# Gate and up products of a decoder layer's two SwiGLU FFNs with the tokens on the partitions

## The chip, the cores and the metric

The kernel runs on one core of a Trainium2 chip, as one launch. The metric is the time of one execution on the device in microseconds, the median of several runs. Engines: PE is TensorE's matmul, PEld its weight load (the load of the stationary operand), DVE is VectorE, ACT is ScalarE, POOL is GpSimd, SP is SyncE, whose queue issues the DMAs.

## What is computed

One decoder layer on 256 tokens of width 2048, in float32: a SwiGLU FFN (half step), a token mixer, a second SwiGLU FFN (half step). Each sub-layer has an RMSNorm with shift and scale ahead of it, an RMSNorm with a gate behind it, and a residual.

```python
def swiglu(h, w_gate, w_up, w_down):
    return (jax.nn.silu(h @ w_gate) * (h @ w_up)) @ w_down

mod = (jax.nn.silu(c) @ w_ada[l] + b_ada[l]).reshape(b_, N_SUBLAYERS, N_MOD, D_MODEL)

def sublayer(x_res, j, fn, coef):
    shift, scale, gate = mod[:, j, 0], mod[:, j, 1], mod[:, j, 2]
    h = rms_norm(x_res, g_pre[l, j]) * (1.0 + scale[:, None, :]) + shift[:, None, :]
    y = rms_norm(fn(h), g_post[l, j])
    return x_res + coef * gate[:, None, :] * y
...
x = sublayer(x, 0, ffn(0), 0.5)
x = sublayer(x, 1, mixer, 1.0)
x = sublayer(x, 2, ffn(1), 0.5)
```

w_gate and w_up are 2048 x 5632, w_down is 5632 x 2048, for each of the two FFNs. w_ada, from which the shifts, scales and gates come, is 2048 x 18432.

## The kernel before

Products are made in three parts. Every operand is split into a high part (rounded to fp32r by a cast) and a low part (what the cast left), and `mm3` (lines 308 to 311) sums high x high, high x low and low x high in PSUM. The activations h lie transposed in SBUF as `hh` and `hl`: 128 partitions by 16 k's by 256 tokens. A weight tile is two k's by 512 columns: `load_w` (line 277) loads it over SP's queue into one of 8 `raw` buffers, `split_w` casts it on ScalarE to `wh` (line 290) and subtracts on VectorE to `wl` (line 291), with 4 buffers each. `w_tiles` (line 295) hands out the tiles of a product; after each tile it calls `pump`, which takes one step of the first of the `pending` generators (evacuations and the like), and lets a side generator step, which loads the next piece of w_ada and sums it on VectorE (line 170).

An FFN works in 11 blocks of 512 columns of w_gate and w_up, taken together in three supers of 4, 4 and 3 blocks, each followed by its part of the down products. A block needs two products, gate and up, each with 8 weight tiles. `proj_t` (line 319) makes them with the output channels on the partitions: the weight tile is the stationary operand, 128 columns at a time, and h moves with its 256 tokens; for one k that is 4 x 3 matmuls of 256 columns into two PSUM banks. `proj_tok` (line 333) is the other form: h is stationary, 128 tokens at a time, and the weight tile moves with 512 columns, 2 x 3 matmuls for a k. The projections of the mixer go by `proj_tok`, but for the two that the convolution reads. In the FFNs only the first block of the second FFN does, since its products are begun while half of the tokens are still in work.

The first FFN begins before h is complete: blocks 0 to 4 get their first quarter of the k's, blocks 5 and 6 a half, block 7 three quarters, and `spill` (line 649) copies each of these sums out of PSUM (line 651). Between them the generator `First` makes shift and scale of the next quarter. The blocks are finished later, and `swiglu_sum` (line 514) adds the spilled part. Block 8 keeps its banks.

SwiGLU's result g must have the channels on the partitions, since the down products use it as the stationary operand. `swiglu_evac` (line 505) takes the silu of the gate's bank, multiplies it by the up's bank (line 509) and splits the result into g (lines 342, 343), one bank per pump. `swiglu_tok` (line 532) does it for the wide block: silu and product of both banks (lines 537, 538), then, at the next two pumps, four transposes each on TensorE against an identity (line 546) into a PSUM bank, and the split out of that bank.

The order of each engine's instructions comes from a scheduler that follows the order in which the code is written and lets an engine go on with later work whose operands and buffers are free. PSUM has 8 banks in one pool, small tiles `t` have 6 buffers.

Of the kernel before, what the change touches and what calls it, by code (L numbers as in the profile page):

```python
# [9 lines left out]
F32R = mybir.dt.float32r  # L10
AF = mybir.ActivationFunctionType
# [21 lines left out]
def tile_layer(  # L33
# [35 lines left out]
    def ps():  # L69
        return psp.tile([P, 512], F32, tag="ps", name=nm("ps"))  # L70
# [237 lines left out]
    def mm3(o, lh, ll, rh, rl, start, stop):  # L308
        nc.tensor.matmul(o, lh, rh, start=start, stop=False, skip_group_check=True)  # L309
        nc.tensor.matmul(o, lh, rl, start=False, stop=False, skip_group_check=True)  # L310
        nc.tensor.matmul(o, ll, rh, start=False, stop=stop, skip_group_check=True)  # L311
# [4 lines left out]
        slots = [Slot((P, 2, 2, 512), F32R) for _ in range(n - nw)]  # L316
        return list(w_tiles(src, segs, c0, [None] * min(n, nw) + [s_.t for s_ in slots])), slots

    def proj_t(src, c0, segs=FULL, banks=None, first=0):

        banks = banks or [ps(), ps()]
        last = segs[-1][0] + segs[-1][1] - 1
        for k, wh, wl in w_tiles(src, segs, c0):
            for m in range(4):
                o = banks[m // 2][:, (m % 2) * S:(m % 2 + 1) * S]
                mm3(o, wh[:, m * P:(m + 1) * P], wl[:, m * P:(m + 1) * P],
                    hh[:, k, :], hl[:, k, :], k == first and m % 2 == 0, k == last)
        return banks

    def tok_mm(k, wh, wl, t, bank):  # L330
        mm3(bank, hh[:, k, t * P:(t + 1) * P], hl[:, k, t * P:(t + 1) * P], wh, wl, k == 0, k == NK - 1)

    def proj_tok(src, c0, begun=None, w=512):

        banks, done = begun or ([ps(), ps()], 0)
        for k, wh, wl in w_tiles(src, FULL[done:], c0, w=w):
            for t in range(NT):
                tok_mm(k, wh, wl, t, banks[t][:, 0:w])
        return banks

    def split_act(dh, dl, src):
# [160 lines left out]
        return banks, 2  # L502


    def swiglu_evac(g, gb, ub):
        for i in range(2):
            sg, gt = t2(), t2()
            nc.scalar.activation(sg, gb[i], AF.Silu)
            nc.vector.tensor_tensor(out=gt, in0=sg, in1=ub[i], op=ALU.mult)
            split_act(g.t[:, 0, 2 * i:2 * i + 2, :], g.t[:, 1, 2 * i:2 * i + 2, :],  # L510
                      gt.rearrange("p (k s) -> p k s", s=S))
            yield

    def swiglu_sum(gb, ub, part):

        pv = part.t.rearrange("p k s -> p (k s)")
        gts = []
        for i in range(2):
            sg, gt = t2(), t2()
            nc.vector.tensor_tensor(out=sg, in0=pv[:, i * 512:(i + 1) * 512], in1=gb[i], op=ALU.add)  # L520
            nc.scalar.activation(sg, sg, AF.Silu)
            nc.vector.tensor_tensor(out=gt, in0=pv[:, 1024 + i * 512:1024 + (i + 1) * 512], in1=ub[i], op=ALU.add)
            nc.vector.tensor_tensor(out=gt, in0=sg, in1=gt, op=ALU.mult)
            gts.append(gt)
        part.free()
        g = Slot((P, 2, 4, S), F32R)
        for i in range(2):
            split_act(g.t[:, 0, 2 * i:2 * i + 2, :], g.t[:, 1, 2 * i:2 * i + 2, :],
                      gts[i].rearrange("p (k s) -> p k s", s=S))
        return g  # L530

    def swiglu_tok(g, gb, ub):

        gts = []
        for t in range(NT):
            sg, gt = t2(), t2()
            nc.scalar.activation(sg, gb[t], AF.Silu)
            nc.vector.tensor_tensor(out=gt, in0=sg, in1=ub[t], op=ALU.mult)
            gts.append(gt)
        yield  # L540
        for i in range(2):
            pg = ps()
            for j in range(2):
                for t in range(NT):
                    m = 2 * i + j
                    nc.tensor.transpose(pg[:, j * S + t * P:j * S + (t + 1) * P], gts[t][:, m * P:(m + 1) * P], ident)
            split_act(g.t[:, 0, 2 * i:2 * i + 2, :], g.t[:, 1, 2 * i:2 * i + 2, :],
                      pg.rearrange("p (k s) -> p k s", s=S))
            yield

    def ffn(idx, supers, begun, xin, nxt, nxt_src=None, nxt_c0=None, nxt_w=512):

        y = None
        yp = [parts() for _ in range(NT)]

        def evac_y(si, q, t, bank):
            ys = y[t].t[:, q * 512:(q + 1) * 512]
            if si == 0:
                nc.scalar.copy(ys, bank)
            else:  # L560
                nc.vector.tensor_tensor(out=ys, in0=ys, in1=bank, op=ALU.add)
            if si == len(supers) - 1:
                sumsq(yp[t], q, ys)

        for si, blocks in enumerate(supers):
            gs = []
            n = len(blocks)
            for b, segs, part, banks in blocks:
                if si == 0 and begun is not None and not gs:
                    gb = proj_tok(w_ff_gate[idx], b * FB, begun)  # L570
                    ub = proj_tok(w_ff_up[idx], b * FB)
                elif part is not None:
                    gb = proj_t(w_ff_gate[idx], b * FB, segs, None, segs[0][0])
                    ub = proj_t(w_ff_up[idx], b * FB, segs, None, segs[0][0])
                    flush()
                    gs.append(swiglu_sum(gb, ub, part))
                    continue
                else:
                    gb = proj_t(w_ff_gate[idx], b * FB, segs, banks and banks[0])
                    ub = proj_t(w_ff_up[idx], b * FB, segs, banks and banks[1])  # L580
                flush()
                gs.append(Slot((P, 2, 4, S), F32R))
                ev = swiglu_tok if si == 0 and begun is not None and len(gs) == 1 else swiglu_evac
                pending.append(ev(gs[-1], gb, ub))
            if y is None:
                y = [Slot((P, D)) for _ in range(NT)] if xin[0].__class__ is Half else [Half(t) for t in range(NT)]
            rows = [(4 * i, 4, 4 * b[0]) for i, b in enumerate(blocks)]

            def mms(k, wh, wl, t):
                g = gs[k // 4].t  # L590
                mm3(banks[t], g[:, 0, k % 4, t * P:(t + 1) * P], g[:, 1, k % 4, t * P:(t + 1) * P],
                    wh, wl, k == 0, k == 4 * n - 1)

            for q in range(4):
                banks = [ps(), ps()]
                if si == len(supers) - 1 and q == 2:
                    for s_ in xin:
                        s_.t
                if si == len(supers) - 1 and q == 3:
                    flush()  # L600
                    if side[0] is not None:
                        side[0].drain()
                    early = early_w(nxt_src, nxt_c0, nxt_w)
                    kept, slots = hold(w_ff_down[idx], rows, q * 512, NW if nxt is None else 3)

                    def last_mm(t):
                        for k, wh, wl in kept:
                            mms(k, wh, wl, t)

                    return boundary(last_mm, lambda t: evac_y(si, q, t, banks[t]), lambda t: times_gg(y, t, q), xin, y, yp, slots + gs,  # L610
                                    early, 1, nxt, nxt_src, nxt_c0, nxt_w)
                else:
                    for k, wh, wl in w_tiles(w_ff_down[idx], rows, q * 512):
                        for t in range(NT):
                            mms(k, wh, wl, t)
                    for t in range(NT):
                        later(evac_y, si, q, t, banks[t])
                        if si == len(supers) - 1:
                            later(times_gg, y, t, q)
            if si < len(supers) - 1:  # L620
                for g in gs:
                    g.free()
# [67 lines left out]
    for bs, n in (((0, 1, 2, 3, 4), 1), ((5, 6), 2), ((7,), 3)):  # L690
        first.until(n - 1)
        for b in bs:
            part = Slot((P, 8, S))
            supers[0 if n > 1 else 1 if b < 4 else 2].append((b, FULL[n:], part, None))
            for u in range(2):
                pending.append(spill(part, u, proj_t(gate_up[u], b * FB, FULL[:n])))
        first.rate = 1.0 if n == 1 else 0.67
    first.until(2)
    banks = [proj_t(gate_up[u], 8 * FB, FULL[:3]) for u in range(2)]
    supers[0].insert(0, (8, FULL[3:], None, banks))  # L700
    first.until(3)
    flush()
# [411 lines left out]
```

## Time and profile before

| | |
|---|---|
| median of 3 runs | 1909.85 us (1909.17 to 1909.91) |
| the profiled execution | 1910.18 us |
| its span, first to last instruction | 1908.4 us |
| PE / PEld / DVE / ACT busy | 97% / 90% / 71% / 45% |
| moved by DMA | 500.31 MB, mean 262 GB/s |

The span is what the trace covers; the little around it belongs to the execution. The first FFN goes to about 800 us, the mixer to about 1150 us, the second FFN to the end. A group of instructions is told by line, engine, operation and the names of the tiles, out<-in, followed by partitions x elements. A matmul's row shows its whole passage through the array, so rows of neighbouring matmuls overlap: the distance of their starts tells how fast they go.

### The profile page before, as it was taken

The numbers are of one execution on the slowest core, as the hardware profiler recorded it, in microseconds if no ns is written. First come the engines' busy times: TensorE is split into PE (matmuls) and PEld (weight loads), VectorE is DVE, ScalarE is ACT, GpSimd is POOL, SyncE is SP. The second block draws the span as 40 slices with busy tenths as digits, with TensorE's granted clock in tenths as the row PEclk, the third lists the DMA queues.
The fourth block names the chain that finished last, engine by engine and source line by source line (L and its number), as shares of the span: only waits on it lengthen the run. The fifth ranks groups of instructions, "written<-read, shape, count | busy, mean of one in ns | idle before, by whom it ended". The sixth has DMA issues, their size and how long they took to land.

```text
span 1908.4 us, 30747 instructions
## 1 busy us (share of the span) xinstructions
PE 1859.7 (97%) x12357; PEld 1726.7 (90%) x12357; DVE 1356.1 (71%) x1472; ACT 854.9 (45%) x1059; POOL 17.3 (1%) x40
## 2 busy tenths in 40 slices
PE   3999999999999999999999999999999999999998
PEld 2999998899988998799988887999889999899996
DVE  7787788778888878868898986555555555555455
ACT  3554444444443444554645446343444444334443
POOL 0000000000000000000000000000000000000000
PEclk9999999999999999999999999999999999999999
DMA  9999889888899998668688994776676676677652
GB/s 352 340 321 332 286 294 320 312 294 311 298 326 318 349 309 292 227 207 278 223 282 305 367 336 135 218 213 209 226 230 207 214 216 209 224 224 214 181 186 96
DMA packets 232646, 500.31 MB, mean 262 GB/s; under 512 B 16828, under 2 KB 28332, under 8 KB 231992
## 3 DMA queue, kind: packets, MB, share of 16 engines
q1 hardware_dynamic: 232504, 498.36, 77.7%
q8 instruction: 96, 1.57, 0.3%
q14 instruction: 46, 0.38, 0.1%
HBM read 496.19 MB, written 2.10 MB: 261 GB/s over the span
## 4 chain that ended last, share of the span: by engine, by line
PE 88%; issue 8%; DVE 2%; POOL 1%; ACT 0%; DMA 0%; SPq 0%; POOLq 0%; DVEq 0%; ACTq 0%
PE ps L309 29%; PE ps L310 29%; PE ps L311 29%; DVE acc L170 1%; PE ps L181 0%; DMA t<-in_g_pre_dram 0%; POOL rstd L360 0%; DVE wl L291 0%; PE ps L901 0%; PE ps L409 0%; ACT t L371 0%; POOL brs L779 0%; ACT hh L342 0%; PE ps L205 0%; PE ps L206 0%
## 5 line engine op out<-in xcount | busy, mean ns | idle before, releaser
L291 DVE TENSOR_TENSOR wl<-raw,wh 128x1024 fp32r<-128x1024 f32 (+2 forms) x637 | 768.7, 1210 | 488.8 <-ACT wh L290 488.4
L290 ACT CAST wh<-raw 128x1024 fp32r<-128x1024 f32 (+2 forms) x637 | 660.5, 1041 | 882.4 <-PE ps L310 466.8
L309 PE MATMUL ps<-hh,wh 128*128 128x256 f32 x2816 | 800.2, 284 | 3.7 <-ACT hh L342 3.0
L310 PE MATMUL ps<-hl,wh 128*128 128x256 f32 x2816 | 798.0, 284 | 0.0
L311 PE MATMUL ps<-hh,wl 128*128 128x256 f32 x2816 | 797.3, 283 | 0.0
L309 PEld LDWEIGHTS ps<-hh,wh 128*128 128x128 f32 x2816 | 541.6, 192 | 5.4 <-ACT hh L342 3.6
L310 PEld LDWEIGHTS ps<-hl,wh 128*128 128x128 f32 x2816 | 541.9, 192 | 1.0 <-issue 0.5
L311 PEld LDWEIGHTS ps<-hh,wl 128*128 128x128 f32 x2816 | 541.3, 192 | 0.0
L170 DVE SCALAR_TENSOR_TENSOR acc<-raw,cs,acc 128x1024 f32<-128x1024 f32 x270 | 345.1, 1278 | 0.5
L309 PE MATMUL ps<-wh,big 128*128 128x512 f32 x804 | 314.2, 391 | 0.0
L311 PE MATMUL ps<-wh,big 128*128 128x512 f32 x804 | 313.0, 389 | 0.0
L310 PE MATMUL ps<-wl,big 128*128 128x512 f32 x804 | 312.9, 389 | 0.0
L311 PEld LDWEIGHTS ps<-wh,big 128*128 128x128 f32 x804 | 150.9, 188 | 31.7
L309 PEld LDWEIGHTS ps<-wh,big 128*128 128x128 f32 x804 | 151.0, 188 | 30.9
L310 PEld LDWEIGHTS ps<-wl,big 128*128 128x128 f32 x804 | 151.0, 188 | 30.5
L309 PE MATMUL ps<-wh,hh 128*128 128x512 f32 (+2 forms) x336 | 126.1, 376 | 0.0
L310 PE MATMUL ps<-wl,hh 128*128 128x512 f32 (+2 forms) x336 | 124.8, 372 | 0.6 <-DVE wl L291 0.6
L311 PE MATMUL ps<-wh,hl 128*128 128x512 f32 (+2 forms) x336 | 124.8, 372 | 0.0
L310 PEld LDWEIGHTS ps<-wl,hh 128*128 128x128 f32 x336 | 63.4, 189 | 8.2 <-DVE wl L291 1.3
L311 PEld LDWEIGHTS ps<-wh,hl 128*128 128x128 f32 x336 | 63.1, 188 | 7.5
L309 PEld LDWEIGHTS ps<-wh,hh 128*128 128x128 f32 x336 | 63.2, 188 | 7.0 <-ACT hh L342 0.2
L651 ACT COPY big<-ps 128x512 f32<-128x512 f32 x32 | 18.8, 589 | 47.4 <-PE ps L311 45.7
(195 smaller groups left out, 715.7 us busy)
## 6 DMA issues: line engine op xcount, KB each, us to landing
raw<-in_w_ada_dram SPq DMA_DIRECT2D x224, 512.0 KB
raw<-in_w_ff_gate_dram SPq DMA_DIRECT2D x176, 512.0 KB
raw<-in_w_ff_up_dram SPq DMA_DIRECT2D x176, 512.0 KB
raw<-in_w_ff_down_dram SPq DMA_DIRECT2D x176, 512.0 KB
raw<-in_w_ada_dram SPq DMA_DIRECT2D x128, 256.0 KB
raw<-in_w_in_dram SPq DMA_DIRECT2D x48, 512.0 KB
raw<-in_w_out_dram SPq DMA_DIRECT2D x32, 512.0 KB
raw<-in_w_in_dram SPq DMA_DIRECT2D x24, 412.0 KB
```

Of the source, the lines that this page charges most:

```text
L170: ins = nc.vector.scalar_tensor_tensor(a, raw[:, j, :, :], cs[:, k:k + 1], a, op0=ALU.mult, op1=ALU.add)
L290: behind(nc.scalar.copy(wh, rawv), floor[1])
L291: last_split[0] = nc.vector.tensor_tensor(out=wl, in0=rawv, in1=wh.bitcast(F32), op=ALU.subtract)
L309: nc.tensor.matmul(o, lh, rh, start=start, stop=False, skip_group_check=True)
L310: nc.tensor.matmul(o, lh, rl, start=False, stop=False, skip_group_check=True)
L311: nc.tensor.matmul(o, ll, rh, start=False, stop=stop, skip_group_check=True)
L651: nc.scalar.copy(part.t.rearrange("p k s -> p (k s)")[:, u * 1024 + i * 512:u * 1024 + (i + 1) * 512], banks[i])
```

## The change

All gate and up products go by `proj_tok`, which gets the arguments that `proj_t` had for parts of the k's; `proj_t` is left for the convolution's two projections. `swiglu_evac` and `swiglu_sum` now find a bank with 128 tokens and 512 channels, take silu and product for each half of the tokens, let two pumps pass, and transpose the result in `to_g`, four transposes at each of two pumps, as `swiglu_tok` did after one pump. `spill` gets its banks from `proj_tok`; its code stays.

```diff
-    def proj_t(src, c0, segs=FULL, banks=None, first=0):
+    def proj_t(src, c0):
...
-    def tok_mm(k, wh, wl, t, bank):
-        mm3(bank, hh[:, k, t * P:(t + 1) * P], hl[:, k, t * P:(t + 1) * P], wh, wl, k == 0, k == NK - 1)
+    def tok_mm(k, wh, wl, t, bank, first=0, last=NK - 1):
+        mm3(bank, hh[:, k, t * P:(t + 1) * P], hl[:, k, t * P:(t + 1) * P], wh, wl, k == first, k == last)
+
+    def proj_tok(src, c0, begun=None, w=512, segs=FULL, banks=None, first=0):
+
+        if begun is not None:
+            banks, segs = begun[0], FULL[begun[1]:]
+        banks = banks or [ps(), ps()]
+        last = segs[-1][0] + segs[-1][1] - 1
+        for k, wh, wl in w_tiles(src, segs, c0, w=w):
             for t in range(NT):
-                tok_mm(k, wh, wl, t, banks[t][:, 0:w])
+                tok_mm(k, wh, wl, t, banks[t][:, 0:w], first, last)
...
-    def swiglu_tok(g, gb, ub):
-
-        gts = []
-        for t in range(NT):
-            sg, gt = t2(), t2()
-            nc.scalar.activation(sg, gb[t], AF.Silu)
-            nc.vector.tensor_tensor(out=gt, in0=sg, in1=ub[t], op=ALU.mult)
-            gts.append(gt)
-        yield
+    def to_g(g, gts):
         for i in range(2):
             pg = ps()
             for j in range(2):
...
+    def swiglu_evac(g, gb, ub):
+        gts = []
+        for t in range(NT):
+            sg, gt = t2(), t2()
+            nc.scalar.activation(sg, gb[t], AF.Silu)
+            nc.vector.tensor_tensor(out=gt, in0=sg, in1=ub[t], op=ALU.mult)
+            gts.append(gt)
+        yield
+        yield
+        yield from to_g(g, gts)
+
+    def swiglu_sum(gb, ub, part):
...
+        part.free()
+        g = Slot((P, 2, 4, S), F32R)
+
+        def rest():
+            yield
+            yield
+            yield from to_g(g, gts)
+
+        pending.append(rest())
+        return g
...
                 elif part is not None:
-                    gb = proj_t(w_ff_gate[idx], b * FB, segs, None, segs[0][0])
-                    ub = proj_t(w_ff_up[idx], b * FB, segs, None, segs[0][0])
+                    gb = proj_tok(w_ff_gate[idx], b * FB, segs=segs, first=segs[0][0])
+                    ub = proj_tok(w_ff_up[idx], b * FB, segs=segs, first=segs[0][0])
...
-                    gb = proj_t(w_ff_gate[idx], b * FB, segs, banks and banks[0])
-                    ub = proj_t(w_ff_up[idx], b * FB, segs, banks and banks[1])
+                    gb = proj_tok(w_ff_gate[idx], b * FB, segs=segs, banks=banks and banks[0])
+                    ub = proj_tok(w_ff_up[idx], b * FB, segs=segs, banks=banks and banks[1])
                 flush()
                 gs.append(Slot((P, 2, 4, S), F32R))
-                ev = swiglu_tok if si == 0 and begun is not None and len(gs) == 1 else swiglu_evac
-                pending.append(ev(gs[-1], gb, ub))
+                pending.append(swiglu_evac(gs[-1], gb, ub))
...
-                pending.append(spill(part, u, proj_t(gate_up[u], b * FB, FULL[:n])))
+                pending.append(spill(part, u, proj_tok(gate_up[u], b * FB, segs=FULL[:n])))
...
-    banks = [proj_t(gate_up[u], 8 * FB, FULL[:3]) for u in range(2)]
+    banks = [proj_tok(gate_up[u], 8 * FB, segs=FULL[:3]) for u in range(2)]
```

Two places show how the instructions move. The first is on TensorE in the second FFN, at the third weight tile of the third block's gate product, where the second block's result is due. Before, it is a row of narrow products, `wh_12655` being that tile:

```order
L309 MATMUL ps_12580<-hh,wh_12655 128x256
L310 MATMUL ps_12580<-hl,wh_12655 128x256
L311 MATMUL ps_12580<-hh,wl_12656 128x256
L309 MATMUL ps_12580<-hh,wh_12655 128x256
L310 MATMUL ps_12580<-hl,wh_12655 128x256
L311 MATMUL ps_12580<-hh,wl_12656 128x256
L309 MATMUL ps_12579<-hh,wh_12685 128x256
L310 MATMUL ps_12579<-hl,wh_12685 128x256
L311 MATMUL ps_12579<-hh,wl_12686 128x256
L309 MATMUL ps_12579<-hh,wh_12685 128x256
```

With the change (`wh_10433` is the same tile, `t_2066` and `t_2068` SwiGLU's result for the two halves of the tokens):

```order
L309 MATMUL ps_10386<-wh_10433,hh 128x512
L310 MATMUL ps_10386<-wl_10434,hh 128x512
L311 MATMUL ps_10386<-wh_10433,hl 128x512
L513 MATMUL ps_10449<-ident,t_2066_10406 128x128
L513 MATMUL ps_10449<-ident,t_2068_10410 128x128
L513 MATMUL ps_10449<-ident,t_2066_10406 128x128
L513 MATMUL ps_10449<-ident,t_2068_10410 128x128
L309 MATMUL ps_10385<-wh_10458,hh 128x512
L310 MATMUL ps_10385<-wl_10459,hh 128x512
L311 MATMUL ps_10385<-wh_10458,hl 128x512
L309 MATMUL ps_10386<-wh_10458,hh 128x512
```

The last products of the tile stand in fewer rows, and four transposes come between them and the next tile. TensorE has 8303 rows in all where it had 12167, 3864 fewer.

The second place is on ScalarE around the same tile. Before, with the cast of `wh_12655` in the second row and the two casts of g out of `t`:

```order
L290 CAST wh_12619<-raw_12617 128x1024
L290 CAST wh_12655<-raw_12653 128x1024
L508 ACTIVATE t_2048_12647<-ps_12064 128x512
L290 CAST wh_12685<-raw_12683 128x1024
L342 CAST big_12578<-t_2044_12612 128x512
L342 CAST big_12578<-t_2049_12648 128x512
L290 CAST wh_12718<-raw_12716 128x1024
L290 CAST wh_12748<-raw_12746 128x1024
L290 CAST wh_12778<-raw_12776 128x1024
L290 CAST wh_12808<-raw_12806 128x1024
```

With the change (the rows of `split_act` are now line 344, those of silu line 522):

```order
L290 CAST wh_10415<-raw_10413 128x1024
L290 CAST wh_10433<-raw_10431 128x1024
L522 ACTIVATE t_2067_10409<-ps_10062 128x512
L290 CAST wh_10458<-raw_10456 128x1024
L290 CAST wh_10486<-raw_10484 128x1024
L290 CAST wh_10504<-raw_10502 128x1024
L290 CAST wh_10522<-raw_10520 128x1024
L344 CAST big_10384<-ps_10449 128x512
L290 CAST wh_10540<-raw_10538 128x1024
L344 CAST big_10384<-ps_10474 128x512
```

The silu stands in the same row; the first cast of g, now out of a PSUM bank, has moved behind the weight casts of four later tiles, and its second one behind a fifth. ScalarE, VectorE and SP have as many rows as before (983, 1425 and 979).

## Rows read from the trace of the kernel before

**Rows 1.** The page, parts 1 and 4.

```profile
PE 1859.7 (97%) x12357; PEld 1726.7 (90%) x12357; DVE 1356.1 (71%) x1472; ACT 854.9 (45%) x1059; POOL 17.3 (1%) x40
...
PE 88%; issue 8%; DVE 2%; POOL 1%; ACT 0%; DMA 0%; SPq 0%; POOLq 0%; DVEq 0%; ACTq 0%
PE ps L309 29%; PE ps L310 29%; PE ps L311 29%; DVE acc L170 1%; PE ps L181 0%; DMA t<-in_g_pre_dram 0%; POOL rstd L360 0%; DVE wl L291 0%; PE ps L901 0%; PE ps L409 0%; ACT t L371 0%; POOL brs L779 0%; ACT hh L342 0%; PE ps L205 0%; PE ps L206 0%
```

**Rows 2.** Busy time by stretch: us, each engine, clock, DMA share, GB/s.

```profile
40.00:215.00 175.00, 175.00 (x1442) 174.97 (x1442) 135.19 (x129) 82.24 (x103) 0.00 (x0) 1.00 0.94 329
...
290.00:380.00 90.00, 90.00 (x411) 74.67 (x410) 70.67 (x69) 39.90 (x44) 0.00 (x0) 1.00 0.91 320
380.00:520.00 140.00, 140.00 (x1166) 139.83 (x1166) 112.80 (x119) 58.77 (x62) 0.00 (x0) 1.00 0.88 300
...
1425.00:1605.00 180.00, 180.00 (x1499) 179.83 (x1498) 99.36 (x91) 73.17 (x77) 0.00 (x0) 1.00 0.68 212
```

**Rows 3.** ScalarE's timeline, second FFN; in brackets idle us and what ended it.

```profile
1249.73 1.05 ACT L290 CAST wh<-raw 128x1024 fp32r<-128x1024 f32 x1 [1.83 <-PE ps L310]
```

**Rows 4.** TensorE's timeline, a gate or up product: start us, us, what; first and 97th.

```profile
1223.81 0.28 PE L310 MATMUL ps<-hl,wh 128*128 128x256 f32 x1
...
1235.33 0.28 PE L310 MATMUL ps<-hl,wh 128*128 128x256 f32 x1
```

**Rows 5.** Groups by form: busy us, mean ns, idle us before and its releasers.

```profile
L309 PE MATMUL ps<-hh,wh 128*128 128x256 f32 x2816 | 800.2, 284 | 3.7 <-ACT hh L342 3.0 <-ACT wh L290 0.6
```

**Rows 6.** The same view, output-gate projection, first and 36th.

```profile
999.77 0.39 PE L309 MATMUL ps<-wh,hh 128*128 128x512 f32 x1
...
1007.70 0.39 PE L311 MATMUL ps<-wh,hl 128*128 128x512 f32 x1
```

**Rows 7.** The same view around the existing transposes.

```profile
1202.54 0.28 PE L311 MATMUL ps<-hh,wl 128*128 128x256 f32 x1
1202.66 0.60 PE L546 MATMUL ps<-ident,t 128*128 128x128 f32 x4
1203.01 0.36 PE L309 MATMUL ps<-hh,wh 128*128 128x256 f32 x1
1203.21 0.28 PE L310 MATMUL ps<-hl,wh 128*128 128x256 f32 x1
```

**Rows 8.** The same view around four transposes among down products.

```profile
298.81 0.60 PE L181 MATMUL ps<-ident,acc 128*128 128x128 f32 x4
...
299.47 0.39 PE L310 MATMUL ps<-wl,big 128*128 128x512 f32 x1
```

**Rows 9.** The same view around four transposes of a normalization.

```profile
818.22 0.60 PE L409 MATMUL ps<-ident,t 128*128 128x128 f32 x4
...
819.04 0.35 PE L310 MATMUL ps<-wl,hh 128*128 128x410 f32 x1
819.23 0.35 PE L309 MATMUL ps<-wh,hh 128*128 128x410 f32 x1
```

**Rows 10.** VectorE's timeline ahead of the existing transposes.

```profile
1196.62 1.28 DVE L538 TENSOR_TENSOR t<-t,ps 128x512 f32<-128x512 f32 x2
```

**Rows 11.** Groups by form: splitting SwiGLU's result out of SBUF and PSUM.

```profile
L343 DVE TENSOR_TENSOR big<-t,big 128x512 fp32r<-128x512 f32 x42 | 28.0, 685 | 0.0
L342 ACT CAST big<-t 128x512 fp32r<-128x512 f32 x42 | 25.2, 618 | 4.6 <-DVE t L523 3.4 <-DVE t L522 0.8 <-DVE t L509 0.4
...
L343 DVE TENSOR_TENSOR big<-ps,big 128x512 fp32r<-128x512 f32 x10 | 6.8, 682 | 0.9 <-ACT big L342 0.9
...
L342 ACT CAST big<-ps 128x512 fp32r<-128x512 f32 x10 | 5.8, 578 | 0.0
```

**Rows 12.** Busy time by stretch, as rows 2.

```profile
20.00:30.00 10.00, 0.00 (x0) 0.00 (x0) 9.71 (x9) 0.00 (x0) 0.00 (x0) 1.00 1.06 387
```

**Rows 13.** ScalarE's timeline, first FFN.

```profile
116.06 1.06 ACT L290 CAST wh<-raw 128x1024 fp32r<-128x1024 f32 x1 [1.77 <-DMA raw<-in_w_ff_up_dram]
118.78 1.05 ACT L290 CAST wh<-raw 128x1024 fp32r<-128x1024 f32 x1 [1.67 <-DMA raw<-in_w_ff_gate_dram]
```

More of the change, by code (lines that the diff above doesn't have):

```diff
@@ L317, in hold @@
         return list(w_tiles(src, segs, c0, [None] * min(n, nw) + [s_.t for s_ in slots])), slots
-    def proj_t(src, c0, segs=FULL, banks=None, first=0):
-        banks = banks or [ps(), ps()]
-        last = segs[-1][0] + segs[-1][1] - 1
-        for k, wh, wl in w_tiles(src, segs, c0):
+    def proj_t(src, c0):
+        banks = [ps(), ps()]
+        for k, wh, wl in w_tiles(src, FULL, c0):
             for m in range(4):
@@ L326, in proj_t @@
                 mm3(o, wh[:, m * P:(m + 1) * P], wl[:, m * P:(m + 1) * P],
-                    hh[:, k, :], hl[:, k, :], k == first and m % 2 == 0, k == last)
+                    hh[:, k, :], hl[:, k, :], k == 0 and m % 2 == 0, k == NK - 1)
         return banks
-    def tok_mm(k, wh, wl, t, bank):
-        mm3(bank, hh[:, k, t * P:(t + 1) * P], hl[:, k, t * P:(t + 1) * P], wh, wl, k == 0, k == NK - 1)
-    def proj_tok(src, c0, begun=None, w=512):
-        banks, done = begun or ([ps(), ps()], 0)
-        for k, wh, wl in w_tiles(src, FULL[done:], c0, w=w):
+    def tok_mm(k, wh, wl, t, bank, first=0, last=NK - 1):
[6 more added lines that the diff above has]
+        for k, wh, wl in w_tiles(src, segs, c0, w=w):
             for t in range(NT):
-                tok_mm(k, wh, wl, t, banks[t][:, 0:w])
+                tok_mm(k, wh, wl, t, banks[t][:, 0:w], first, last)
         return banks
@@ L502, in boundary @@
         return banks, 2
-    def swiglu_evac(g, gb, ub):
-        for i in range(2):
-            sg, gt = t2(), t2()
[L508 to L511, printed above, removed]
-            yield
-    def swiglu_sum(gb, ub, part):
-        pv = part.t.rearrange("p k s -> p (k s)")
-        gts = []
[L518 to L523, printed above, removed]
-            gts.append(gt)
[L525 to L530, printed above, removed]
-    def swiglu_tok(g, gb, ub):
-        gts = []
-        for t in range(NT):
-            sg, gt = t2(), t2()
-            nc.scalar.activation(sg, gb[t], AF.Silu)
-            nc.vector.tensor_tensor(out=gt, in0=sg, in1=ub[t], op=ALU.mult)
-            gts.append(gt)
-        yield
+    def to_g(g, gts):
         for i in range(2):
@@ L549, in swiglu_tok @@
             yield
+    def swiglu_evac(g, gb, ub):
[9 more added lines that the diff above has]
+    def swiglu_sum(gb, ub, part):
+        pv = part.t.rearrange("p k s -> p (k s)")
+        gts = []
+        for t in range(NT):
+            sg, gt = t2(), t2()
+            nc.vector.tensor_tensor(out=sg, in0=pv[:, t * 512:(t + 1) * 512], in1=gb[t], op=ALU.add)
+            nc.scalar.activation(sg, sg, AF.Silu)
+            nc.vector.tensor_tensor(out=gt, in0=pv[:, 1024 + t * 512:1024 + (t + 1) * 512], in1=ub[t], op=ALU.add)
+            nc.vector.tensor_tensor(out=gt, in0=sg, in1=gt, op=ALU.mult)
+            gts.append(gt)
+        part.free()
[6 more added lines that the diff above has]
+        return g
     def ffn(idx, supers, begun, xin, nxt, nxt_src=None, nxt_c0=None, nxt_w=512):
```

## The prediction

> **What bounds the kernel now.** I read the busy table and the chain first [rows 1]. The chain that ends last runs 88% on TensorE, nearly all of it in the three lines of mm3, which leaves little to the other engines. Busy time alone would mislead, since a matmul's shown time overlaps the next one's, so I went to the stages [rows 2]. From 40 us on, the gate and up products keep TensorE busy without a hole: 175.00 of 175 us, 140.00 of 140, 180.00 of 180. VectorE stands at 77%, 81% and 55% there, DMA at 0.94, 0.88 and 0.68; the granted clock is 1.00 in all. In the products of a gate block ScalarE's cast of the next weight tile waits for TensorE to give back a buffer [rows 3]; the supply waits for the products, not the reverse. What counts is therefore the distance from one matmul's start to the next.
>
> **The narrow products.** In a gate or up product of today, 97 matmuls in a row of 256 columns start between 1223.81 and 1235.33 us [rows 4]: 11.52 / 96 = 0.1200 us each. Their weight loads fill PEld too (179.83 of 180 us [rows 2]). The list by form has 2816 of them on each of the three lines [rows 5]. Of these 8448, the two convolution projections, which stay as they are, make 2 x 16 x 4 x 3 = 384; the change touches 8064.
>
> **The wide products.** The kernel already has the form that the change brings: the projection of the output gate holds h and moves 512 columns of wh or wl. 36 of these start between 999.77 and 1007.70 us [rows 6]: 7.93 / 35 = 0.2266 us each. Where two narrow ones take 0.2400 us, one wide one takes 0.2266. The columns are the same; 13.4 ns go with the instruction that is left out. 8064 narrow become 4032 wide: 4032 x 13.4 ns = **54.0 us less**, if TensorE stays the bound. Per weight tile of two k's that is 2.88 against 2.72 us, 0.16 less, in 176 tiles of the first FFN and 160 of the second, whose first block is wide already (336 tiles x 12 = 4032).
>
> Here a rule of the Trainium skill speaks against the change: "TensorE: Matmul & The Clock Gate", section "Back-to-back issue gap", gives N / 2.4 + 2.5 ns for a matmul of N columns. By it two narrow ones take 218.3 ns and a wide one 215.8, an estimate of 2.5 ns saved per pair or 10.1 us in all, which is less than the transposes below cost. The rows give 120.0 and 226.6 ns, and the sum goes by them.
>
> **The transposes.** 21 blocks get 8 transposes each, 168 in 42 groups of four; 8064 - 4032 - 168 = 3864 fewer matmuls. The kernel does the very same thing once, in the second FFN's first block [rows 7]: the four start at 1202.66, the next product at 1203.01, and the one behind that at 1203.21 instead of 0.12 later. 0.55 less the usual 0.12 makes 0.43 us per group. In front of wide products, from the four's start to the second product behind them, it is 0.66 less one wide pitch, the same again [rows 8]. A group that was less lucky took 0.82 - 0.19 = 0.63 us [rows 9]. I take 0.44, the common value rounded up: 42 x 0.44 = **18.5 us more**, with 42 x 0.63 = 26.5 us as the upper end and 42 x 0.43 = 18.1 as the lower; nothing excuses TensorE from issuing them, so they aren't free.
>
> The same page of the Trainium skill has, in "Part 4: PE-mode transpose", some 275 ns for one transpose in a kernel; as a price for each of 168 that would be an estimated 46 us. The rows show 0.60 us for four together, since they overlap, and the sum goes by that.
>
> **What the transposes wait for.** SwiGLU's products must be done before them. In that existing place VectorE's two multiplications end at 1197.90 [rows 10] and the transposes start at 1202.66: 4.8 us to spare with one pump between. The change puts two pumps ahead, one weight tile or 2.7 us more. ScalarE's order shows the result's cast behind four later weight casts, so it holds up none that TensorE is about to need. I cost these waits at nothing; if the cover went, the products of the next block would stand behind the transposes on TensorE.
>
> **ScalarE, VectorE, DMA.** The number of instructions of each stays the same, the queue of loads too. The result is now cast and subtracted out of PSUM in place of SBUF: 578 against 618 ns and 682 against 685 [rows 11], 42 each, some 2 us less on engines off the path. In the blocks that add a spilled part, the two casts and subtractions move from the block's end to behind the next block's third and fourth tile, which thins a burst. Each block takes two more PSUM banks for a moment, out of eight: gate, up and the next gate hold six at most, and gate's and up's are read before the transposes start. I cost all of it at nothing.
>
> **Where the supply may give out.** In the second FFN nothing is near: DMA 0.68, VectorE 55% [rows 2]. In the first, the stretch of down products from 290 to 380 us runs at the wide pace already, with 320 GB/s, DMA at 0.91, VectorE at 79% and TensorE busy for all of 90.00 us; the gate products there would ask the same. The tight place is 40 to 215 us, where the sums for shift and scale come in between: 329 GB/s now. Its 60 tiles would take 9.6 us less, which asks 329 x 175 / 165.4 = 348 GB/s; ten microseconds before the first product went at 387 [rows 12]. Inside it, two of ScalarE's casts already wait for the DMA, at 116.06 and 118.78 us, 2.72 us apart [rows 13]: there the supply has just the wide pace and not more. For the 16 tiles around it I strike half of the gain, 16 x 0.16 / 2 = **1.3 us more**; the bounds are 0 and all 9.6.
>
> **The sum.** -54.0 + 18.5 + 1.3 = -34.2 us. The profiled execution took 1910.2 us with a span of 1908.4; it would take 1876.0. It stands 0.3 above the median, so I say **1875.7**. With no loss of supply and 0.43 a group it is 1874.0, and half of the 3.7 us that TensorE idles ahead of narrow products [rows 5] might go too: 1872. With 0.63 a group it is 1883.7.
>
> **The rivals.** First, the supply is the bound in the first FFN. If all 9.6 us before 215 us are lost, the time is 1875.7 + 8.3 = 1884.0. If the whole first FFN gives nothing, 28.2 us go, and its 22 groups of transposes (9.7 us) hide in the waits: 1875.7 - 1.3 + 28.2 - 9.7 = 1892.9. For it speaks the DMA share of 0.94 and the two waits; against it 387 GB/s and the stretch from 290 to 380 us. Chance 0.11, of which 0.07 up to 1888.
>
> Second, and on the other side: the transposes wait for VectorE, and TensorE, which takes its instructions in order, stands with them. The place is the next block's third tile; the gain left per group is 34.2 / 42 = 0.81 us, so a wait longer than that in each makes the change slower. With 2.7 us, one tile, in each of the 42: 42 x 2.7 = 113 us, 1989; with 1.2 us, 1926. Against it: the 4.8 us of [rows 10] and one more pump. Chance 0.03.
>
> Third, time goes by columns and not by instructions: the 512-column products in this place take twice the narrow ones. Then nothing pays for the transposes: 1909.9 + 18.5 + 1.3 = 1929.7; it decides from where 4032 pairs save less than 18.5 + 1.3 = 19.8 us, 4.9 ns each, that is from a wide pitch of 0.2351 us on. For it: those wide rows come from another stage. Against it: operands, types and widths are the same. Chance 0.02. The gap that the Trainium skill gives (above) would come out near this rival, at an estimated 1919.6.
>
> That the change doesn't do what it says is not left open: its order has 3864 fewer matmuls.
>
> **How the numbers follow.** The forecast's own case, 1872 to 1883, has 0.83; the first rival 0.11; the second 0.03; the third 0.02; a gain that vanishes for another reason 0.01. The range from 1872 to 1886 holds the first case and the milder half of the first rival, just under 0.9; I don't cut it closer, since 1884 is a named end. 0.2% is 3.8 us, about what a measurement can tell from no change. Faster 0.94, same 0.01, slower 0.05.
>
> **What would show it.** In the new profile: wide gate products at 0.2266 us; 42 groups of four transposes, each with the next product's start 0.35 us behind; TensorE busy without holes from 40 us to the first boundary; the DMA share before 215 us near 0.99; the second FFN shorter by 160 x 0.16 - 20 x 0.44 = 16.8 us. Wrong if ScalarE's casts wait for DMA over more than that one stretch, if the transposes show idle time of TensorE ended by VectorE, or if the wide pitch is above 0.23 us.

## The result and the profile after

The changed kernel takes **1877.97 us** (1877.42 to 1878.43, 4 runs) against 1909.78 beside it: 31.8 us less, a ratio of 0.9834 with a 95% interval of 0.9818 to 0.9849. The forecast was 1875.7, the range 1872 to 1886. Its profiled execution took 1877.58 us with a span of 1875.9.

The page of the changed kernel, the lines that answer to [rows 1]:

```profile
PE 1827.3 (97%) x8493; PEld 1530.3 (82%) x8493; DVE 1355.3 (72%) x1472; ACT 853.4 (45%) x1059; POOL 17.2 (1%) x40
...
PE 88%; issue 8%; DVE 2%; ACT 1%; POOL 1%; DMA 0%; SPq 0%; DVEq 0%; POOLq 0%; ACTq 0%
PE ps L309 29%; PE ps L311 28%; PE ps L310 28%; DVE acc L170 1%; PE ps L513 1%; PE ps L181 0%; DMA t<-in_g_pre_dram 0%; PE ps L411 0%; POOL rstd L362 0%; DVE wl L291 0%; ACT t L373 0%; PE ps L900 0%; POOL brs L778 0%; ACT hh L344 0%; PE ps L205 0%
```

3864 matmul rows fewer, PEld down from 90% to 82%, and the chain still runs on TensorE's three lines. VectorE's and ScalarE's busy time is what it was; the same work stands in a shorter span. TensorE's groups by form, answering to [rows 5] (busy us, mean ns, idle us before):

```profile
L309 PE MATMUL ps<-wh,hh 128*128 128x512 f32 x1528 | 598.4, 394 | 3.8 <-DVE t L386 2.4 <-ACT hh L344 0.7 <-ACT wh L290 0.6
...
L309 PE MATMUL ps<-hh,wh 128*128 128x256 f32 x128 | 37.6, 294 | 0.0
...
L513 PE MATMUL ps<-ident,t 128*128 128x128 f32 x176 | 26.3, 272 | 0.0
```

1528 wide ones per line: the 184 of before, and 1344 that replace 2688 narrow ones. 128 narrow ones stay with the convolution. The transposes (line 513) number 176, 168 of them new, and TensorE never idles ahead of them. Busy time by stretch, answering to [rows 2] (us of PE, PEld, DVE, ACT, POOL with their counts; clock, DMA share, GB/s), all three in gate and up products:

```profile
40.00:205.00 165.00, 165.00 (x737) 135.77 (x736) 134.53 (x129) 82.30 (x103) 0.00 (x0) 1.00 0.97 347
369.00:504.00 135.00, 135.00 (x616) 111.72 (x615) 112.26 (x117) 58.18 (x63) 0.00 (x0) 1.00 0.89 308
1402.00:1579.00 177.00, 177.00 (x794) 146.49 (x793) 100.39 (x92) 75.98 (x81) 0.00 (x0) 1.00 0.72 221
```

TensorE has no hole in any of them. In the first stretch the DMA moves 347 GB/s at a share of 0.97; the prediction had asked 348 of it and said 0.99. PEld, full before, is at 112 of 135 us. Now TensorE's timeline in a gate product of the second FFN and around new transposes, answering to [rows 4], [rows 6] and [rows 7]; the first two lines are the first and the 20th of an unbroken row:

```profile
1449.62 0.39 PE L310 MATMUL ps<-wl,hh 128*128 128x512 f32 x1
...
1453.93 0.39 PE L311 MATMUL ps<-wh,hl 128*128 128x512 f32 x1
1454.16 0.60 PE L513 MATMUL ps<-ident,t 128*128 128x128 f32 x4
1454.51 0.48 PE L309 MATMUL ps<-wh,hh 128*128 128x512 f32 x1
1454.83 0.40 PE L310 MATMUL ps<-wl,hh 128*128 128x512 f32 x1
1455.06 0.40 PE L311 MATMUL ps<-wh,hl 128*128 128x512 f32 x1
1455.30 0.40 PE L309 MATMUL ps<-wh,hh 128*128 128x512 f32 x1
1455.53 0.39 PE L310 MATMUL ps<-wl,hh 128*128 128x512 f32 x1
...
1457.37 0.60 PE L513 MATMUL ps<-ident,t 128*128 128x128 f32 x4
```

(1453.93 - 1449.62) / 19 = 0.2268 us from start to start, the wide pace of [rows 6]. The four transposes hold the next product to 1454.51 and the one behind it to 1454.83: 0.67 less a pitch of 0.227 is 0.44 us. What I hadn't seen is in the lines below: 0.23, 0.24, 0.23 us. The products behind a group of transposes start some nanoseconds late for about ten rows, until the pitch is back at 0.227. The last line is the block's second group, 12 products behind the first: 3.21 - 12 x 0.2267 = 0.49 us is what the first group cost in all. Counted so, the 44 groups cost 0.46 or 0.49 us each, 0.47 in the mean, of which 0.03 are the late starts. Among narrow products the late starts are missing: behind the group at 1202.66 of [rows 7] the next one starts at 1205.97, 24 products later, and 3.31 - 24 x 0.12 = 0.43 us.

Where the time went is read from four landmarks. TensorE's timeline before, at the transposes for the last quarter's shift and scale, those at the end of the first FFN, and those at the end of the mixer:

```profile
215.25 1.04 PE L181 MATMUL ps<-ident,acc 128*128 128x128 f32 x8
...
801.92 1.03 PE L392 MATMUL ps<-ident,t 128*128 128x128 f32 x8
...
1146.95 1.09 PE L392 MATMUL ps<-ident,t 128*128 128x128 f32 x8 [1.04 <-DVE t L384]
```

The same after:

```profile
205.39 1.04 PE L181 MATMUL ps<-ident,acc 128*128 128x128 f32 x8
...
784.08 1.03 PE L394 MATMUL ps<-ident,t 128*128 128x128 f32 x8
...
1129.12 1.09 PE L394 MATMUL ps<-ident,t 128*128 128x128 f32 x8 [1.04 <-DVE t L386]
```

9.9 us are won up to the first, 17.8 up to the second and as many up to the third: the mixer is untouched. The spans end 32.5 us apart, so the second FFN brings the other 14.7.

About 1 us of the first 9.9 isn't the change's. In every profile the first products, from 37.7 us on, start about half as fast as later ones (narrow ones 0.21 us apart, wide ones 0.43), and the full pace comes at 45.4 us in the profile before and at 42.5 in the one after. The run with the change in the second FFN alone (below) has the first FFN of before and its full pace from 42.9 us on. The first two landmarks there:

```profile
214.10 1.04 PE L181 MATMUL ps<-ident,acc 128*128 128x128 f32 x8
...
800.77 1.03 PE L392 MATMUL ps<-ident,t 128*128 128x128 f32 x8
```

Against these 8.7 us are won up to the first landmark and 16.7 up to the second.

### The profile page after: what moved, and what is told of

Read it like the earlier page. It is cut to its first block, busy times and chain, and to the rows that moved or that the text cites. A ratio compares the mean times of both kernels' runs of the same rounds, so it can differ in the third digit from the quotient of the medians.

```text
span 1875.9 us, 23017 instructions
## 1 busy us (share of the span) xinstructions
PE 1827.3 (97%) x8493; PEld 1530.3 (82%) x8493; DVE 1355.3 (72%) x1472; ACT 853.4 (45%) x1059; POOL 17.2 (1%) x40
## 4 chain that ended last, share of the span: by engine, by line
PE 88%; issue 8%; DVE 2%; ACT 1%; POOL 1%; DMA 0%; SPq 0%; DVEq 0%; POOLq 0%; ACTq 0%
PE ps L309 29%; PE ps L311 28%; PE ps L310 28%; DVE acc L170 1%; PE ps L513 1%; PE ps L181 0%; DMA t<-in_g_pre_dram 0%; PE ps L411 0%; POOL rstd L362 0%; DVE wl L291 0%; ACT t L373 0%; PE ps L900 0%; POOL brs L778 0%; ACT hh L344 0%; PE ps L205 0%
## 5 line engine op out<-in xcount | busy, mean ns | idle before, releaser
L309 PE MATMUL ps<-wh,hh 128*128 128x512 f32 (+2 forms) x1680 | 651.6, 390 | 3.8 <-DVE t L386 2.4
L310 PE MATMUL ps<-wl,hh 128*128 128x512 f32 (+2 forms) x1680 | 648.6, 386 | 0.6 <-DVE wl L291 0.6
L311 PE MATMUL ps<-wh,hl 128*128 128x512 f32 (+2 forms) x1680 | 648.7, 386 | 0.0
L309 PEld LDWEIGHTS ps<-wh,hh 128*128 128x128 f32 x1680 | 315.8, 188 | 63.5 <-ACT hh L344 4.1
L310 PEld LDWEIGHTS ps<-wl,hh 128*128 128x128 f32 x1680 | 316.2, 188 | 61.2 <-DVE wl L291 2.6
L311 PEld LDWEIGHTS ps<-wh,hl 128*128 128x128 f32 x1680 | 315.6, 188 | 60.5
L309 PE MATMUL ps<-hh,wh 128*128 128x256 f32 x128 | 37.6, 294 | 0.0
L345 DVE TENSOR_TENSOR big<-ps,big 128x512 fp32r<-128x512 f32 x52 | 35.6, 684 | 1.2 <-ACT big L344 1.2
L311 PE MATMUL ps<-hh,wl 128*128 128x256 f32 x128 | 36.2, 283 | 0.0
L310 PE MATMUL ps<-hl,wh 128*128 128x256 f32 x128 | 36.2, 283 | 0.0
```

Source lines behind the costliest of these rows:

```text
L345: return nc.vector.tensor_tensor(out=dl, in0=src, in1=dh.bitcast(F32), op=ALU.subtract), act
```

## The experiments

The theory: TensorE bounds the kernel; each matmul left out is worth its fixed share of the pitch, and the transposes are paid in full on TensorE. Its rivals: the gain lies in which operand is held still, not in the width; the first FFN's supply takes part of the gain; the transposes wait for VectorE.

**Without the transposes.** SwiGLU's result is split as it lies, so the down products read a g in the wrong layout.

```diff
-            pg = ps()
-            for j in range(2):
-                for t in range(NT):
...
             split_act(g.t[:, 0, 2 * i:2 * i + 2, :], g.t[:, 1, 2 * i:2 * i + 2, :],
-                      pg.rearrange("p (k s) -> p k s", s=S))
+                      gts[i].rearrange("p (k s) -> p k s", s=S))
```

> The changed kernel without the 44 groups of four transposes: SwiGLU's result is split as it lies, tokens on the partitions, so the down products read it in the wrong layout. Everything else stays. If each group holds TensorE for 0.44 us as predicted, 1878.0 - 44 x 0.44 = 1858.6 us. If the slower wide products that the new trace shows right behind each group belong to its price, 0.49 us each, 1856.4. If the supply of the first FFN is what keeps the gain small, TensorE would wait for weights instead and the time stays above 1868.

Measured: 1856.37 us (1856.08 to 1856.90), ratio to before 0.9722 (0.9708 to 0.9737). The page:

```profile
PE 1805.0 (97%) x8317; PEld 1512.2 (82%) x8317; DVE 1353.8 (73%) x1472; ACT 856.8 (46%) x1059; POOL 17.3 (1%) x40
```

176 matmuls fewer than the changed kernel and 21.6 us: 21.6 / 44 = 0.49 us a group. The medians of two kernels can differ by about 1 us for reasons told above (the start) and below (a boundary), which is 0.02 a group. The landmarks that enclose the 22 groups of the first FFN leave that out. In this run they are:

```profile
205.62 1.03 PE L181 MATMUL ps<-ident,acc 128*128 128x128 f32 x8
...
773.75 1.03 PE L394 MATMUL ps<-ident,t 128*128 128x128 f32 x8
```

From the one to the other it takes 568.1 us, the changed kernel 578.7 (784.08 - 205.39): 10.6 / 22 = 0.48 us a group. The late starts belong to the price. The run also shows the other term alone: 1909.4 - 1856.4 = 53.0 us for the width, with the two groups that even the kernel before has taken away too.

**Half the width, roles kept.** Each wide gate or up product, but for those of the second FFN's first block, becomes two of 256 columns, h still held still.

```diff
+                if half:
+                    for c in (0, 256):
+                        mm3(banks[t][:, c:c + 256], hh[:, k, t * P:(t + 1) * P], hl[:, k, t * P:(t + 1) * P],
+                            wh[:, c:c + 256], wl[:, c:c + 256], k == first and c == 0, k == last)
+                    continue
                 tok_mm(k, wh, wl, t, banks[t][:, 0:w], first, last)
```

> The changed kernel with every wide gate and up product (but those of the second FFN's first block) made as two matmuls of 256 columns each, h still stationary: the roles of the operands stay changed, the width goes back. If the price goes by the number of matmuls, 13.4 ns each, the gain of 54 us goes and the transposes stay: 1909.8 + 42 x 0.43 = about 1928 us, and the distance of two starts is 0.120 us. If the gain came from which operand is held, it stays at about 1878.

Measured: 1929.26 us (1928.59 to 1929.46), ratio 1.0103 (1.0086 to 1.0120), slower than before. TensorE's timeline in a gate product, the first and the last of 19 products in a row:

```profile
1724.78 0.28 PE L311 MATMUL ps<-wh,hl 128*128 128x256 f32 x1
...
1726.93 0.28 PE L311 MATMUL ps<-wh,hl 128*128 128x256 f32 x1
```

(1726.93 - 1724.78) / 18 = 0.1194 us, the narrow pace (0.120, within the rounding of the rows) with the roles of the wide kernel. The gain is in the width and not in the roles: 1929.26 - 1877.97 = 51.3 us for 4032 matmuls, 12.7 ns each (13.1 once it is counted that 42 groups cost 0.04 us less among narrow products). The first rival is out.

**No pumps ahead of the transposes.**

```diff
-        yield
-        yield
         yield from to_g(g, gts)
```

(the same in `swiglu_sum`)

> The changed kernel without the two pumps between SwiGLU's products and the transposes: they are due two weight tiles (5.4 us) sooner. By the prediction 7.5 us are to spare, so 2.1 are left: 1878.0 within 1 us, and no idle time of TensorE ahead of the transposes. If the pumps are what hides VectorE, each of 21 blocks stalls TensorE by 1 us or more: 1899 or above.

Measured: 1878.02 us (1877.76 to 1878.14), ratio 0.9835 (0.9820 to 0.9850): no difference from the changed kernel. VectorE's timeline where the margin is thin, the two multiplications of one block:

```profile
1447.12 1.27 DVE L523 TENSOR_TENSOR t<-t,ps 128x512 f32<-128x512 f32 x2
```

and TensorE's, the two groups of transposes that read them:

```profile
1448.91 0.60 PE L513 MATMUL ps<-ident,t 128*128 128x128 f32 x4
...
1452.10 0.60 PE L513 MATMUL ps<-ident,t 128*128 128x128 f32 x4
```

The multiplications end at 1448.39 and the first transposes start at 1448.91. Half a microsecond is left, less than the 2.1 expected, because other work of VectorE stands ahead of the multiplications in this block; the wait never shows. In the first FFN the scheduler itself parts some of the groups, for instance into one transpose at 248.37 us and three at 249.88, with six products between them. The pumps are cover that isn't needed here. The rival in which the transposes wait is out.

**The second FFN alone.** In the kernel before, blocks of the second FFN go by `proj_tok` and `swiglu_tok` with a second pump.

```diff
         yield
+        yield
...
-                    gb = proj_t(w_ff_gate[idx], b * FB, segs, banks and banks[0])
-                    ub = proj_t(w_ff_up[idx], b * FB, segs, banks and banks[1])
+                    if idx == 1:
+                        gb = proj_tok(w_ff_gate[idx], b * FB)
+                        ub = proj_tok(w_ff_up[idx], b * FB)
+                    else:
+                        gb = proj_t(w_ff_gate[idx], b * FB, segs, banks and banks[0])
+                        ub = proj_t(w_ff_up[idx], b * FB, segs, banks and banks[1])
...
-                ev = swiglu_tok if si == 0 and begun is not None and len(gs) == 1 else swiglu_evac
+                ev = swiglu_tok if idx == 1 else swiglu_evac
```

> The kernel before with wide gate and up products and two pumps in the second FFN alone (160 weight tiles, 20 new groups of transposes). By width and transposes alone 160 x 0.161 - 20 x 0.49 = 16.0 us less than before: 1893.8. By the prediction's 0.44 a group, 1893.0. If the clock falls in the boundary ahead of the second FFN, as in the changed kernel's profile, 1.1 us more. If the first FFN gave nothing and the second gave all, 1878.

Measured: 1893.73 us (1893.13 to 1894.34), ratio 0.9917 (0.9903 to 0.9932). 15.7 us of the 31.8 come from the second FFN, and the first brings the other 16.1 (16.7 by the landmarks of this run and the changed kernel). By the sum with 0.48 us a group the first FFN should bring 176 x 0.161 - 22 x 0.48 = 17.8 us, so between 1 and 2 us of it are lost to something else.

It also settles a detail. In the changed kernel's own profile the second FFN brought 14.7 us, 1 less than here. Busy time of TensorE and the granted clock at the boundary ahead of the second FFN, in the changed kernel:

```profile
1127.70:1131.00 3.30, 1.47 (x10) 1.00 0.03 10
1131.00:1133.00 2.00, 1.98 (x5) 0.58 0.00 0
1133.00:1134.70 1.70, 1.70 (x5) 0.50 0.00 0
```

and in this one:

```profile
1144.40:1147.70 3.30, 1.46 (x10) 1.00 0.01 4
1147.70:1150.00 2.30, 2.29 (x10) 1.00 0.00 0
```

In both, TensorE is busy for less than half of 3.3 us while it waits for the second FFN's first h. In the one the granted clock then falls to half of full speed, the lower of the two levels, within the 3.7 us of the two rows behind, and eight products start 0.43 us apart instead of 0.23; in the other it doesn't fall. It fell in two of the eight profiles of this study (the other is that with six buffers, below) and held in six, among them the changed kernel without pumps, which has the same boundary. So it isn't the change's doing: it is worth about 1 us in a single execution. The slow pace at the start (above) is worth as much. It is the same 0.43 us for wide products, though the profile shows a granted clock of 1.00 there, so that it is the clock is not shown. The changed kernel without pumps has its full pace from 45.0 us on, 2.5 later than the changed kernel, loses 1.2 us by it, keeps the clock at the boundary, and ends up with the same span.

**Both groups at one pump.** Eight transposes in a row, once a block.

```diff
             split_act(g.t[:, 0, 2 * i:2 * i + 2, :], g.t[:, 1, 2 * i:2 * i + 2, :],
                       pg.rearrange("p (k s) -> p k s", s=S))
-            yield
+        yield
```

> The changed kernel with both groups of four transposes at one pump, eight in a row, so that wide products are interrupted once a block. The traces show some 0.05 us of slower starts behind each interruption. If they belong to the interruption, 22 x 0.05 = 1.1 us less than the changed kernel: 1876.9. If they belong to each group of four, or if two PSUM banks at once make TensorE wait, 1878.0 or more. The clock at the start and at the boundary moves single executions by about 1 us either way, so the phases of the trace decide rather than the median: a down phase, which holds one block's transposes, would take 89.75 instead of 89.8 and 87.72 instead of 87.77 us.

Measured: 1875.93 us (1875.29 to 1876.52, 5 runs), ratio 0.9825 (0.9812 to 0.9839). TensorE's timeline around one such place:

```profile
1497.10 1.04 PE L513 MATMUL ps<-ident,t 128*128 128x128 f32 x8
1497.90 0.48 PE L309 MATMUL ps<-wh,hh 128*128 128x512 f32 x1
1498.21 0.39 PE L310 MATMUL ps<-wl,hh 128*128 128x512 f32 x1
1498.44 0.39 PE L311 MATMUL ps<-wh,hl 128*128 128x512 f32 x1
1498.67 0.40 PE L309 MATMUL ps<-wh,hh 128*128 128x512 f32 x1
1498.91 0.39 PE L310 MATMUL ps<-wl,hh 128*128 128x512 f32 x1
```

The late starts come once: 0.23, 0.23, 0.24 us behind the interruption, not twice. The span is 1.7 us shorter than the changed kernel's; 1.0 of that is the clock, which held at the boundary here, and the down phases are 0.05 to 0.2 us shorter each, as expected. So it is the fastest of the kernels that keep the transposes. The medians are 2.0 us apart, and the merging explains about 1 of them, which the phases show; the intervals of the two ratios overlap, though the runs' times don't.

**Six buffers for loads.**

```diff
-    rawp = ctx.enter_context(tc.tile_pool(name="rawp", bufs=8))
+    rawp = ctx.enter_context(tc.tile_pool(name="rawp", bufs=6))
```

> The changed kernel with 6 instead of 8 buffers for loaded weights and sums, so that the queue of loads can run less far ahead: how far is the supply from being the bound? If there is room to spare, 1878 to 1880 us, with the loss between 40 and 215 us alone. If the supply just holds, as the prediction's strike of 1.3 us before 215 us supposed, TensorE waits there and in the rest of the first FFN: 1884 or above.

Measured: 1892.36 us (1891.95 to 1892.99), ratio 0.9912 (0.9898 to 0.9925). Neither expectation fits: it is slow, but not in the gate products of the first FFN. Busy time by stretch with six buffers, the stretch up to the last quarter of h and the mixer's output products:

```profile
40.00:205.00 165.00, 162.86 (x715) 131.24 (x715) 133.50 (x127) 81.67 (x102) 0.00 (x0) 1.00 0.95 332
1042.00:1143.00 101.00, 95.19 (x419) 74.39 (x417) 84.24 (x96) 45.61 (x63) 1.17 (x3) 1.00 0.92 318
```

The second of these with eight buffers:

```profile
1037.00:1128.00 91.00, 91.00 (x418) 75.16 (x416) 82.05 (x95) 43.37 (x61) 0.66 (x3) 1.00 0.97 347
```

The first stretch loses 2.1 us inside and ends its phase 4.8 us later than with eight buffers; the gate products from 370 to 720 us lose nothing; the mixer's output products take 9.3 us more, in a stretch that the change doesn't touch. ScalarE's waits for DMA before 215 us, as us in total, times and longest, with six buffers:

```profile
ACT wh L290 <- DMA raw<-in_w_ff_up_dram: 28.9, 21, 2.8
ACT wh L290 <- DMA raw<-in_w_ff_gate_dram: 27.6, 21, 3.2
...
PEld ps L310 <- DVE wl L291: 6.2, 11, 1.1
```

with eight:

```profile
ACT wh L290 <- DMA raw<-in_w_ff_up_dram: 10.8, 8, 2.5
ACT wh L290 <- DMA raw<-in_w_ff_gate_dram: 7.1, 5, 1.7
```

and in the kernel before:

```profile
ACT wh L290 <- DMA raw<-in_w_ff_up_dram: 7.1, 4, 2.6
...
ACT wh L290 <- DMA raw<-in_w_ff_gate_dram: 5.4, 4, 1.7
```

So the supply up to 215 us is nearer to its limit than before (17.9 us of such waits against 12.5), and two buffers fewer are enough to put it on the path. With eight it hardly is. Of the starts of TensorE's products between 46 and 205 us three places stand out, 0.15 to 0.21 us late each, where the low part of a weight comes too late. VectorE's timeline at the last of them:

```profile
148.83 1.27 DVE L170 SCALAR_TENSOR_TENSOR acc<-raw,cs,acc 128x1024 f32<-128x1024 f32 x1
150.03 2.35 DVE L291 TENSOR_TENSOR wl<-raw,wh 128x1024 fp32r<-128x1024 f32 x2
```

and TensorE's:

```profile
151.29 0.50 PE L310 MATMUL ps<-wl,hh 128*128 128x512 f32 x1
```

VectorE makes the first of two wl's from 150.03 to about 151.25, behind a sum for w_ada, and the product that reads it starts at 151.29. Here VectorE's order and not the DMA holds TensorE up; the other two places, at 110.73 and 148.36 us, come behind copies of spilled sums on ScalarE and behind the normalization of the next quarter of h.

## Why the prediction was right

- **The bound.** Right: TensorE has no hole in any gate or up stretch shown, before or after, and the first five experiments moved the time by what they did to TensorE's row of starts; only with fewer buffers does the supply count.
- **The width: 54.0 us.** Right, and some 2 us too high with what is lost in the first FFN, or 0.7 once the 1.3 us for the supply are taken off. The pitch came out at 0.2268 us against 0.2266. Without transposes the kernel is 53.0 us faster than before in the median; less the two groups that it has lost besides, 0.9 us, that leaves 52. That the role of an operand doesn't count was assumed there; the half-width run shows it. The prediction also left open whether the narrow pace is a fixed price for each matmul or a floor set by the weight loads, which fill PEld there. A third width in the trace before speaks against a floor; these are the first and the 40th of a row of products with 410 columns:

```profile
826.26 0.35 PE L309 MATMUL ps<-wh,hh 128*128 128x410 f32 x1
...
833.54 0.35 PE L309 MATMUL ps<-wh,hh 128*128 128x410 f32 x1
```

7.28 / 39 = 0.1867 us. From 512 to 410 columns a column saves (226.7 - 186.7) / 102 = 0.39 ns, from 410 to 256 (186.7 - 120.0) / 154 = 0.43 ns; with a floor the second would be the smaller.
- **The transposes: 18.5 us.** Mis-sized. The step took the group's cost up to the second product behind it, 0.44 us, and that much is there. The late starts of the next ten products were left out; with them a group costs 0.47 to 0.48 us, 42 of them some 20 us, 1.5 more. The rows to see it were in the trace of before, behind other transposes among wide products; the existing place of [rows 7] has narrow products behind it, and there the pitch is back at 0.12 at once.
- **What the transposes wait for: nothing.** Right, and by more than claimed: without both pumps nothing changes.
- **ScalarE, VectorE, banks: nothing.** Nearly: their busy time stayed within 2 us. But where they have other work before 215 us, wl came late at three places, 0.5 us in all; the trace before has none that late.
- **The supply: 1.3 us lost.** Near in size, and partly by luck. Up to the landmark at 214.10 us 8.7 us were won where the 60 tiles without any loss give 9.6: about 1 us is lost. But the step gave it to the DMA, and the three late places, which are half of it, come from the order of ScalarE's and VectorE's work; the rest stays open. The prediction read two waits of ScalarE for the DMA before 215 us; the trace before has eight, from 116 to 162 us, and the one after 13, from 93 to 168. If "that one stretch" among the prediction's signs of being wrong means the 16 tiles around its two waits, the sign came up and did no harm: most of these waits never reach TensorE. The rival in which the first FFN gives nothing is refuted by the second FFN alone, which brings only half of the gain; the six buffers show how thin the cover is.
- **The sum.** With the measured terms, the first of which holds what the first FFN lost, it is -52 + 20 = -32 us, against -31.8 measured; the forecast's -34.2 was 2.4 too much, about 1.5 of it by the transposes and 0.7 by width and supply together. The clock at the boundary takes 1.0 us in the profiled execution, and the pace at the start moves single executions by about as much; how often either happens in the others was not measured.
- **The Trainium skill's rules.** "TensorE: Matmul & The Clock Gate" of the Trainium skill, section "Back-to-back issue gap", gives N / 2.4 + 2.5 ns as the gap of an isolated matmul; the prediction took it as a rule for the stream of this kernel, and by it the changed kernel would be slower than before. The runs decide for a fixed share of some 13 ns a matmul here, not 2.5. For a stream of weight loads and matmuls the same section of the Trainium skill has about 131 ns at 512 columns; the rows show 226.8. The same page of the Trainium skill has about 275 ns for one transpose (of bf16) in "Part 4: PE-mode transpose"; the rows show a duration of 272 ns for these of float32, but 0.47 us on the path for four.

## What to carry to other kernels

Where TensorE has no holes, count matmuls and not only columns: here each one costs about 13 ns beyond its columns, so the form that moves 512 columns takes 5.6% less time than the one that moves 256, and eight transposes a block take back two fifths of that. Take the price of an inserted instruction from starts far enough behind it, among neighbours of the width that it will have, and make few long interruptions rather than many short ones. Before relying on more speed of the bound engine, look at how far ahead the loads run: here two buffers fewer cost 14 us.

## What the runs showed of the hardware that was not expected

Behind transposes, wide products start 0.23 to 0.24 us apart for about ten of them and then 0.227 again; a group of four so costs 0.47 us in the mean among wide products and 0.43 among narrow ones. Why was not tried. And at the boundary ahead of the second FFN, whose code is the same in all these kernels, the granted clock falls to half in one profile and holds in another: 0.58 and 0.50 over 3.7 us in the changed kernel, 1.00 in the run with the second FFN alone, behind 1.47 and 1.46 us of work in 3.3.
